# A decoder block on one core: the pooling gate's projection as seven block products, and loads pinned to program order

## The chip, the cores and the metric

One of the eight cores of one Trainium2 chip runs the whole kernel. The metric is the device time of one execution in microseconds (us). All data are 32-bit floats.

## The reference

The layer takes x (1024 rows of 1024), normalises it to h, projects h by one wide matrix and runs two branches, attention and pooling. The change sits in the pooling branch:

```
h = rms_norm(x, norm_gain) * (1 + scale) + shift         # scale, shift, gate from c
q, k, v, z_a, u, z_b, m_a, m_b = split(h @ w_in)         # eight blocks of 1024 columns
attn   = stick_breaking_attention(q, k, v)               # 16 heads, strictly causal
p_a    = (attn * silu(z_a)) @ w_branch_a
# pooling: trailing mean over 2, 4, 8 or 16 rows (by group of 256 channels) minus the row itself
d      = (cs - cs_shift) / count - u
p_b    = ((d @ pool_w) * pool_scale * silu(z_b)) @ w_branch_b
merged = sigmoid(m_a) * p_a + sigmoid(m_b) * p_b
out    = rms_norm(x + gate * (merged @ w_out), final_gain)
```

The kernel multiplies `pool_w` into the weights of u beforehand, so its `d` is already the pooled value before scale and gate.

## The kernel before

**Stages.** TensorE (PE) works through stages in this order: u (the pooled branch's input, weights already mapped), v, m (for m_b), z (for z_b), b (the product with `w_branch_b`), then attention with the remaining projections woven in, then the two output products. A float product is made of three products of split operands: high by high, high by low, low by high. ScalarE (ACT) casts the high half (fp32r), VectorE (DVE) subtracts it from the source to get the low half, so that each operand block costs one ACT cast and one DVE subtraction before PE can use both halves.

**`seven`.** A 1024x1024x1024 product in 2x2 blocks takes eight block products. Stages v, m and b use a scheme of seven: products p1 to p7 of sums and differences of blocks, 48 matmuls each (4 row tiles x 2 halves q x 2 x 3), into PSUM "chains" of four banks: a chain keeps accumulating over several products (p1, p6, p7, p4 in one; p5, p3 in another; p2 alone). The order of the products is p1, p5, p6, p7, p4, p3, p2. `raw` loads an operand block half (512 KB, two buffers of tag "raw" and two of tag "ar"); `a_s1`, `a_s3`, `a_s4` form the sums on DVE; `a_op` and `b_op` split into halves; `copied` and `added` take partial sums out of PSUM; `final(m, n, j, src)` hands over tile j of output block (m, n): (1,1) after p7, (1,0) after p4, (0,1) after p3, (0,0) after p2. In stage v, `values` casts the tile to halves (tile `vo`, three buffers) and stores it to DRAM `v_d`; in m, `gate_b` applies a sigmoid (tile `sb`) and stores to `sb_d`; in b, `branch` stores to `pb_d`.

**Stage z.** `project` runs z_b as eight column tiles of 48 matmuls (names `wzb`), 384 in all. Beside each tile j, the loop loads `u_d[j]`, forms the trailing-window difference (`load_u`, `make_d`: one to four window additions, one subtraction, two tiny edge operations), multiplies it with silu(z) (`silu`), forms the differences of quarters that stage b needs (t1, t2), and adds one eighth of the modulation gate: a load `wg` of `w_gate` and one DVE product with the row `sg` = silu(c).

**What sets the order.** Each engine runs its instructions strictly in a fixed order. A scheduler picks that order when the program is built, from its own estimates; `tc.keep_in_program_order` forbids it to put an instruction ahead of the one written before it on the same engine. SyncE (SP) issues nearly all transfers, one after the other: a transfer that waits for a semaphore holds back all behind it. In stages v, m, z and b no transfer is pinned before the change, and nothing on PE is.

Of the kernel before, what the change touches and what calls it, by code (L numbers as in the profile page):

```python
# [9 lines left out]
F32 = mybir.dt.float32  # L10
# [5 lines left out]
P = 128  # L16
# [35 lines left out]
def block_kernel(ctx, tc, a, out):  # L52
# [3 lines left out]
    def pool(name, **kw):  # L56
        return tc.tile_pool(name=name, bufs=1, reuse_waits="tile", **kw)
# [9 lines left out]
    def bank(tag, name):  # L67
        return psp.tile([P, 512], F32, tag=tag, bufs=BANKS[tag], name=name)
# [463 lines left out]
    dhls = {}  # L532

    def load_u(j):
        u = dif.tile([P, S + 16], F32, tag="u", bufs=2, name=f"u{j}")
        v.memset(u[:, S:], 0.0)
        nc.sync.dma_start(u[:, :S], u_d[j])
        return u

    def make_d(j, u):  # L540
        win = WINDOWS[j // 2]
        cur, n, step = u, S + 16, 1
        while step < win:
            nxt = dif.tile([P, S + 16], F32, tag="win", bufs=2, name=f"win{j}_{step}")
            n -= step
            v.tensor_add(nxt[:, :n], cur[:, :n], cur[:, step:step + n])
            cur, step = nxt, 2 * step
        t0 = S - win + 1
        d = dif.tile([P, S], F32, tag="d", bufs=5, name=f"d{j}")
        v.scalar_tensor_tensor(d[:, :t0], cur[:, :t0], 1.0 / win, u[:, :t0], ALU.mult, ALU.subtract)  # L550
# [21 lines left out]
    def added(t, src):  # L572
        v.tensor_add(t, src, t)
        return t

    def seven(nm, sums, load, b_of, a_moves, ta, tb, final, direct):

        s2k = sums.tile([P, 4, 512], F32, tag="s2k", bufs=1, name=nm + "s2k")

# [30 lines left out]
            return t  # L610

        chain, keep = {}, {}
        for name in ("p1", "p5", "p6", "p7", "p4", "p3", "p2"):
            c = {"p5": "b", "p3": "b", "p2": "c"}.get(name, "a")
# [14 lines left out]
            for j in range(4):  # L629
                if name == "p1":  # L630
                    keep["s1", j] = copied("s1", 4, j, ps[j])
                elif name == "p6":
                    keep["s2", j] = copied("s2", 4, j, ps[j])
                elif name == "p7":
                    final(1, 1, j, added(copied("s3", 4, j, ps[j]), chain["b"][j]))
                elif name == "p4":
                    final(1, 0, j, ps[j] if direct else copied("s3", 4, j + 4, ps[j]))
                elif name == "p3":
                    final(0, 1, j, added(keep["s2", j], ps[j]))
                elif name == "p2":  # L640
                    final(0, 0, j, added(keep["s1", j], ps[j]))

    with ExitStack() as vps:

        vp = vps.enter_context(pool("vp"))

        tq = [vp.tile([P, 4, 512], F32, name=f"ht{i}") for i in range(4)]

        def hq(k, n, q):
            sl = slice(4 * k + 2 * q, 4 * k + 2 * q + 2), slice(512 * n, 512 * n + 512)  # L650
            return [t[:, sl[0], sl[1]].bitcast(F32) for t in (h_hi, h_lo)]

        def difference(dst, x, y, name):
            tmp = vp.tile([P, 2, 512], F32, tag="tmp", bufs=1, name=name)
# [19 lines left out]
        for i in reversed(range(KB)):  # L674
# [15 lines left out]

        def loads(w):
            def load(t, m, k, q):
                nc.sync.dma_start(t.rearrange("p k c -> p (k c)"), a[w][m, 2 * k + q])
            return load

        def values(m, n, j, src):
# [8 lines left out]
            )  # L705

        def gate_b(m, n, j, src):
            t = vs.tile([P, 512], F32, tag="go", bufs=3, name=f"sb{4 * m + j}_{n}")
            act.activation(t, src, AF.Sigmoid)
# [5 lines left out]
    turns[0] = cycle(("av", "tr", "pj", "z"))  # L715
    diffs = ExitStack()
    dif = diffs.enter_context(pool("dif", side="right"))

    pbs = ExitStack()
    pb = pbs.enter_context(pool("pb"))  # L720
    gb = pb.tile([P, KB, S], F32, name="gb")
    t1 = pb.tile([P, 4, 512], F32, name="t1")
    t2 = pb.tile([P, 4, 512], F32, name="t2")
    gate = pb.tile([P, KB], F32, name="gate")
    bias = pb.tile([P, KB], F32, name="gbias")
    nc.sync.dma_start(bias, a["b_gate"])
    sg = pb.tile([P, D], F32, name="sg")

    def part(src, k, n, q):
        return src[:, 4 * k + 2 * q:4 * k + 2 * q + 2, 512 * n:512 * n + 512]  # L730

    for j in range(KB):
        if j not in dhls:
            make_d(j, load_u(j))

        def silu(sh, ps):
            z = gb[:, j, sh * 512:sh * 512 + 512]
            act.activation(z, ps, AF.Silu)
            v.scalar_tensor_tensor(z, dhls[j][:, sh * 512:sh * 512 + 512], psc_v[:, j:j + 1], z, ALU.mult, ALU.mult)

        project(CZB + j, f"wzb{j}", silu, act, v)
        if j < 4:
            v.tensor_sub(t1[:, j], gb[:, j, 512:], gb[:, j, :512])
        else:
            v.tensor_sub(t2[:, j - 4], gb[:, j, 512:], t1[:, j - 4])
            v.tensor_sub(gb[:, j - 4, 512:], gb[:, j, 512:], gb[:, j - 4, 512:])
        if j == 0:
            nc.sync.dma_start(sg, a["c_row"].broadcast_to([P, D]))
            act.activation(sg, sg, AF.Silu)
        wg = pb.tile([P, D], F32, tag="wg", bufs=1, name=f"wg{j}")  # L750
        nc.sync.dma_start(wg, a["w_gate"][j])
        v.scalar_tensor_tensor(wg, wg, 1.0, sg, ALU.mult, ALU.mult, accum_out=gate[:, j:j + 1])
        del dhls[j]
    v.tensor_add(gate, gate, bias)
    nc.sync.dma_start(g_d[0].rearrange("(k p) -> p k", p=P), gate)
    diffs.close()

    sums = pbs.enter_context(pool("sums", side="right"))

    def load_b_w(t, m, k, q):  # L760
        r0 = (4 * k + 2 * q) * P
        nc.sync.dma_start(t, a["w_branch_b"][r0:r0 + 2 * P, 512 * m:512 * m + 512].rearrange("(k p) c -> p k c", p=P))

    def g_parts(name, q):
        if name in ("p5", "p6"):
            src = k2(t1 if name == "p5" else t2, q)
        elif name == "p4":
            src = k2(t2, q)
            v.tensor_sub(src, part(gb, 1, 0, q), src)
        else:  # L770
            src = part(gb, *dict(p1=(0, 0), p7=(0, 1), p3=(1, 1), p2=(1, 0))[name], q)
        return b_op(src, pb, 3, f"{name}b{q}")
# [10 lines left out]
    with pool("at") as at:  # L783
# [439 lines left out]
```

## Time and profile before

| | us |
|---|---|
| three runs | 1189.05, 1190.29, 1190.63; median 1190.29 |
| the profiled execution, device time | 1187.59 |
| its span, first to last instruction | 1185.8 |
| stage v in it | 129 to 205 |
| stage m | 205 to 281 |
| stage z | 281 to 368 |
| stage b | 368 to 445 |

Two views matter below. Groups of instructions give, for each line and kind, the count, the total busy time and the mean of one in ns, then the engine's idle time just before and what ended it. The list of transfers gives, for each, the queue that issues it, the count, its size and the median time from issue to landing. "SPq" is SP as an issuer of transfers. A matmul's mean (390 ns) is its length in the pipeline; the total divided by the count is what one adds.

### The profile page before, as it was taken

The numbers are of one execution on the slowest core, as the hardware profiler recorded it, in microseconds if no ns is written. First come the engines' busy times: TensorE is split into PE (matmuls) and PEld (weight loads), VectorE is DVE, ScalarE is ACT, GpSimd is POOL, SyncE is SP. The second block draws the span as 40 slices with busy tenths as digits, with TensorE's granted clock in tenths as the row PEclk, the third lists the DMA queues.
The fourth block names the chain that finished last, engine by engine and source line by source line (L and its number), as shares of the span: only waits on it lengthen the run. The fifth ranks groups of instructions, "written<-read, shape, count | busy, mean of one in ns | idle before, by whom it ended". The sixth has DMA issues, their size and how long they took to land.

```text
span 1185.8 us, 15373 instructions
## 1 busy us (share of the span) xinstructions
PE 1169.2 (99%) x5602; PEld 975.0 (82%) x5602; DVE 832.4 (70%) x1072; ACT 588.3 (50%) x1137; POOL 216.7 (18%) x248
## 2 busy tenths in 40 slices
PE   8999999999999999999999999999999999999997
PEld 7888888888888887888888888887888888888876
DVE  5767467555996651878788788879787973894653
ACT  5561355454313532667666666666666764232111
POOL 1000000000000004124234242443343622000001
PEclk9999999999999999999999999999999999999999
DMA  9651529546535257322333142423333126984622
GB/s 349 257 193 62 180 103 318 187 162 234 200 103 176 97 179 222 79 81 91 84 98 90 62 121 54 135 62 103 94 88 99 37 72 208 349 280 157 213 70 73
DMA packets 74750, 172.49 MB, mean 145 GB/s; under 512 B 9393, under 2 KB 22833, under 8 KB 72498
## 3 DMA queue, kind: packets, MB, share of 16 engines
q1 hardware_dynamic: 68770, 160.82, 41.6%
q10 hardware_dynamic: 5904, 10.68, 2.5%
q8 instruction: 44, 0.72, 0.3%
q14 instruction: 32, 0.26, 0.1%
HBM read 121.14 MB, written 33.56 MB: 130 GB/s over the span
## 4 chain that ended last, share of the span: by engine, by line
PE 84%; DVE 7%; DMA 3%; issue 3%; ACT 2%; SPq 0%; POOL 0%; POOLq 0%; DVEq 0%; ACTq 0%
PE p L101 24%; PE wzb L101 7%; PE mp L101 6%; PE vp L101 6%; PE bp L101 6%; PE o L101 6%; PE pa L101 5%; PE u L101 5%; PE z L101 5%; PE av L101 4%; PE wt L101 4%; PE ua L101 3%; DVE om L942 2%; DVE be L101 2%; PE wm L101 1%
## 5 line engine op out<-in xcount | busy, mean ns | idle before, releaser
L101 PE MATMUL p<-hT,w 128*128 128x512 f32 x1536 | 392.7, 392 | 1.3 <-DVE klo L101 1.3
L101 PEld LDWEIGHTS p<-hT,w 128*128 128x128 f32 x1536 | 283.0, 188 | 59.5 <-DVE klo L101 1.7
L942 DVE TENSOR_TENSOR_SCAN om<-om,eye 128x511 f32<-128x511 f32 (+7 forms) x128 | 184.0, 1442 | 68.9 <-ACT om L938 68.3
L149 POOL TENSOR_TENSOR w<-w_raw,w 128x256 fp32r<-128x256 f32 x124 | 124.8, 1037 | 571.5 <-ACT w L146 571.5
L938 ACT ACTIVATE om<-z 128x512 f32<-128x512 f32 (+2 forms) x192 | 95.0, 495 | 109.2 <-PE z L101 46.8
L962 DVE TENSOR_TENSOR wt<-wt,wt 128x512 fp32r<-128x512 f32 (+1 forms) x160 | 99.0, 619 | 15.7 <-ACT wt L961 14.7
L101 PE MATMUL av<-wt,vv 128*128 128x512 f32 x320 | 106.0, 412 | 0.1
L961 ACT CAST wt<-wt 128x512 fp32r<-128x512 f32 (+1 forms) x160 | 88.2, 551 | 35.0 <-PE wt L101 34.8
L101 DVE TENSOR_TENSOR be<-be,om 128x512 f32<-128x512 f32 (+7 forms) x128 | 98.5, 775 | 0.0
L101 PE MATMUL wt<-ident,be 128*128 128x128 f32 x576 | 90.3, 274 | 3.9 <-DVE wt L962 3.1
L939 ACT ACTIVATE be<-z 128x512 f32<-128x512 f32 (+2 forms) x192 | 94.0, 489 | 0.0
L101 PE MATMUL pa<-ga,wa 128*128 128x512 f32 x384 | 89.9, 390 | 0.9 <-DVE s L1115 0.8
L101 PE MATMUL o<-wo,mhl 128*128 128x512 f32 (+1 forms) x408 | 89.6, 377 | 0.0
L101 PE MATMUL wzb<-hT,wzb 128*128 128x512 f32 x384 | 87.2, 389 | 0.0
L101 PEld LDWEIGHTS pa<-ga,wa 128*128 128x128 f32 x384 | 71.9, 188 | 16.5 <-issue 1.2
L101 PEld LDWEIGHTS o<-wo,mhl 128*128 128x128 f32 x408 | 73.5, 188 | 14.1
L101 PEld LDWEIGHTS wt<-ident,be 128*128 128x128 f32 x576 | 69.5, 140 | 18.7 <-DVE wt L962 6.2
L101 PEld LDWEIGHTS wzb<-hT,wzb 128*128 128x128 f32 x384 | 72.1, 188 | 15.0
L991 POOL TENSOR_TENSOR tp<-tp,tl 128x256 f32<-128x256 f32 x32 | 38.1, 1190 | 153.9 <-DVE tp L988 153.9
L101 PE MATMUL z<-kl,q 128*128 128x512 f32 (+2 forms) x192 | 65.5, 341 | 0.0
L101 PE MATMUL z<-kh,q 128*128 128x512 f32 (+2 forms) x192 | 64.1, 334 | 0.0
L101 PE MATMUL u<-hT,wg 128*128 128x512 f32 x240 | 55.5, 391 | 0.0
(265 smaller groups left out, 1650.0 us busy)
## 6 DMA issues: line engine op xcount, KB each, us to landing
w_raw<-in_w_in SPq DMA_DIRECT2D x32, 512.0 KB, 3.5
v_d<-vo SPq DMA_DIRECT2D x16, 512.0 KB, 4.2
vv<-v_d SPq DMA_DIRECT2D x8, 1024.0 KB, 6.3
wa_raw<-in_w_branch_a SPq DMA_DIRECT2D x16, 512.0 KB, 4.7
wa<-in_w_mod SPq DMA_DIRECT2D x7, 1024.0 KB, 7.4
kh<-kh SPq DMA_DIRECT2D x48, 128.0 KB, 2.3
va<-in_w_v SPq DMA_DIRECT2D x10, 512.0 KB, 4.0
ma<-in_w_mb SPq DMA_DIRECT2D x10, 512.0 KB, 4.4
```

Source lines behind the costliest of these rows:

```text
L101: ins = op(*args, **kw)
L149: gp.tensor_tensor(hl[:, 1, es], raw[:, es], hl[:, 0, es].bitcast(F32), op=ALU.subtract)
L938: act.activation(om[:, 1 + b0:1 + b0 + n], zp[:, :n], AF.Sigmoid, scale=-0.125)
L939: act.activation(be[:, b0:b0 + n], zp[:, :n], AF.Sigmoid, scale=0.125)
L942: v.tensor_tensor_scan(om[:, 1:W], om[:, 1:W], eye[:, :W - 1], 0.0, ALU.mult, ALU.max)
L961: act.copy(wt[:, 0, :off], pt[:, :off])
L962: v.tensor_sub(wt[:, 1, :off], pt[:, :off], wt[:, 0, :off].bitcast(F32))
L991: gp.tensor_add(tp, tp, tl)
```

## The change

1. Stage z becomes a call of `seven` with the weights laid out for it (`w_zb`), and `gate_z` as its `final`. The silu output goes to four quarter tiles `gq`; three of them reuse tiles of differences of h whose last product is done.
2. The order of the seven products becomes p1, p2, p5, p6, p7, p4, p3 in all four stages, so that block (0,0) is handed over second and (0,1) last; p2 takes the four banks that p5 takes after it. All stages use the same banks for the same chains.
3. The pooling differences are made in stages v and m, one after each of four products (`beside`), and stored to a new DRAM tensor `d_d` through GpSimd's queue (POOL); `gate_z` loads them back by tiles `ds` (three buffers).
4. The modulation gate's eight parts go beside the products of stage z.
5. `held` pins the loads of weights, of u and of `w_gate` to program order on SP; so are the stores of `branch` and the loads of v in attention.
6. `sb` has two buffers where it had three.

The diff, cut:

```
+    def held(dst, src):
+        tc.keep_in_program_order(nc.sync.dma_start(dst, src))
 def load_u(j):
-        nc.sync.dma_start(u[:, :S], u_d[j])
+        held(u[:, :S], u_d[j])
 def make_d(j, u):
...
-        dhls[j] = d
+        gp.dma_start(d_d[j], d)
-    def seven(nm, sums, load, b_of, a_moves, ta, tb, final, direct):
+    def seven(nm, sums, load, b_of, a_moves, ta, tb, final, direct, beside={}):
...
-        for name in ("p1", "p5", "p6", "p7", "p4", "p3", "p2"):
+        for name in ("p1", "p2", "p5", "p6", "p7", "p4", "p3"):
...
-                chain[c] = [bank((tb if c == "b" else ta)[j // 2], f"{nm}{name}_{j}") for j in range(4)]
+                chain[c] = [bank((ta if c == "a" else tb)[j // 2], f"{nm}{name}_{j}") for j in range(4)]
...
+            for do in beside.get(name, ()):
+                do()
...
             def load(t, m, k, q):
-                nc.sync.dma_start(t.rearrange("p k c -> p (k c)"), a[w][m, 2 * k + q])
+                held(t.rearrange("p k c -> p (k c)"), a[w][m, 2 * k + q])
...
-        seven("v", vs, loads("w_v"), h_parts("v"), True, ("av", "tr"), ("pj", "z"), values, True)
-        seven("m", vs, loads("w_mb"), h_parts("m"), False, ("pj", "z"), ("av", "tr"), gate_b, True)
+        seven("v", vs, loads("w_v"), h_parts("v"), True, *banks, values, True, pooled(p1=(3,), p6=(2,), p7=(1,), p3=(0,)))
+        seven("m", vs, loads("w_mb"), h_parts("m"), False, *banks, gate_b, True, pooled(p1=(7,), p6=(4,), p7=(6,), p3=(5,)))
+        diffs.close()
...
-        project(CZB + j, f"wzb{j}", silu, act, v)
+            def gate_z(m, n, j, src):
+                ct = 4 * m + j
+                ds = zg.tile([P, 512], F32, tag="ds", bufs=3, name=f"ds{ct}_{n}")
+                nc.sync.dma_start(ds, d_d[ct][:, 512 * n:512 * n + 512])
+                z = gq[m, n][:, j]
+                act.activation(z, src, AF.Silu)
+                v.scalar_tensor_tensor(z, ds, psc_v[:, ct:ct + 1], z, ALU.mult, ALU.mult)
...
+            def modulated(j):
+                wg = zg.tile([P, D], F32, tag="wg", bufs=1, name=f"wg{j}")
+                held(wg, a["w_gate"][j])
+                v.scalar_tensor_tensor(wg, wg, 1.0, sg, ALU.mult, ALU.mult, accum_out=gate[:, j:j + 1])
+            where = dict(p1=(0, 1), p6=(2,), p7=(3, 4), p4=(5,), p3=(6, 7))
+            seven("z", vs, loads("w_zb"), h_parts("z"), False, *banks, gate_z, True, ...)
...
+        seven("b", vs, load_b_w, g_parts, False, *banks, branch, False)
```

Three places show how the order of instructions moves. In the names, `va`, `ma`, `za`, `ba` are the loads of operand blocks of stages v, m, z, b (a11, a12, a21, a22, with `s` or `d` for the copies used in sums; the digit behind is the half q), and the last number counts tiles.

First place, SP in stage v. Before, around the end of p7 and p4:

```order
L693 DMA va22_0_1405<-in_w_v 128x1024
L693 DMA va22_1_1437<-in_w_v 128x1024
L693 DMA va12s_0_1485<-in_w_v 128x1024
L702 DMA v_d_75<-vo4_1_1380 128x4x256
L702 DMA v_d_75<-vo5_1_1387 128x4x256
L693 DMA va12s_1_1515<-in_w_v 128x1024
L702 DMA v_d_75<-vo6_1_1394 128x4x256
L702 DMA v_d_75<-vo7_1_1401 128x4x256
```

The loads of p4 (va22) and p3 (va12s) stand ahead of most of the stores of p7's results. Now, around the end of p2:

```order
L577 DMA va12_1_1213<-in_w_v 128x1024
L712 DMA v_d_75<-vo0_0_1243 128x4x256
L712 DMA v_d_75<-vo1_0_1248 128x4x256
L712 DMA v_d_75<-vo2_0_1253 128x4x256
L712 DMA v_d_75<-vo3_0_1258 128x4x256
L577 DMA va21_0_1266<-in_w_v 128x1024
L577 DMA va22_0_1268<-in_w_v 128x1024
L577 DMA va11s_0_1271<-in_w_v 128x1024
```

The loads for p5 (va21, va22, va11s) stand behind the four stores of p2's results; the same pattern follows p7, p4 and p3.

Second place, SP at the change from stage m to stage z. Before:

```order
L693 DMA ma12_1_2145<-in_w_mb 128x1024
L129 DMA wzb0_raw_2215<-in_w_in 128x1024
L710 DMA sb_d_76<-sb0_1_2097 128x512
L710 DMA sb_d_76<-sb1_1_2101 128x512
L710 DMA sb_d_76<-sb2_1_2105 128x512
L710 DMA sb_d_76<-sb3_1_2109 128x512
L129 DMA wzb1_raw_2290<-in_w_in 128x1024
```

The first weights of stage z are loaded before the stores of p3's results of m. Now:

```order
L720 DMA sb_d_76<-sb3_1_2292 128x512
L577 DMA u5_2295<-u_d_78 128x1024
L744 DMA gbias_2319<-in_b_gate 128x8
L746 DMA sg_2321<-in_c_row 128x1024
L577 DMA za11_0_2329<-in_w_zb 128x1024
L577 DMA za11_1_2358<-in_w_zb 128x1024
```

The first weights (za11) stand behind the last store of stage m, the load of u5 and the load of `sg`, whose place in memory was the differences' work space: it waits for the difference of u5. ACT now has, behind m's last sigmoid:

```order
L719 ACTIVATE sb3_1_2292<-ms2_3_2015 128x512
L747 ACT_TABLE_LOAD
L747 ACTIVATE sg_2321<-sg_2321 128x1024
L559 CAST zp1a0_2331<-za11_0_2329 128x1024
L559 CAST zp1a1_2360<-za11_1_2358 128x1024
```

The cast of the first weights stands behind the table load and silu of `sg`.

Third place, SP at the change from stage z to stage b. Before:

```order
L129 DMA wzb7_raw_2755<-in_w_in 128x1024
L537 DMA u6_2659<-u_d_78 128x1024
L751 DMA wg7_2816<-in_w_gate 128x1024
L762 DMA ba11_0_2830<-in_w_branch_b 128x2x512
L537 DMA u7_2739<-u_d_78 128x1024
L755 DMA g_d_74<-gate_2201 128x8x1
```

The first weights of b (ba11) go ahead of the store of the finished gate `g_d`. Now:

```order
L737 DMA ds3_1_2897<-d_d_79 128x512
L577 DMA wg6_2901<-in_w_gate 128x1024
L577 DMA wg7_2904<-in_w_gate 128x1024
L758 DMA g_d_74<-gate_2318 128x8x1
L577 DMA ba11_0_2919<-in_w_branch_b 128x2x512
L577 DMA ba11_1_2951<-in_w_branch_b 128x2x512
```

They stand behind both last parts of the gate (one buffer `wg`) and behind the store of the finished gate.

More of the change, by code (lines that the diff above doesn't have):

```diff
@@ L81, in block_kernel @@
     u_d = dram.tile([KB, P, S], F32, name="u_d")
+    d_d = dram.tile([KB, P, S], F32, name="d_d")
     ident = idp.tile([P, P], F32, name="ident")
@@ L548, in make_d @@
         t0 = S - win + 1
-        d = dif.tile([P, S], F32, tag="d", bufs=5, name=f"d{j}")
+        d = dif.tile([P, S], F32, tag="d", bufs=2, name=f"d{j}")
         v.scalar_tensor_tensor(d[:, :t0], cur[:, :t0], 1.0 / win, u[:, :t0], ALU.mult, ALU.subtract)
@@ L653, in difference @@
         def difference(dst, x, y, name):
-            tmp = vp.tile([P, 2, 512], F32, tag="tmp", bufs=1, name=name)
+            tmp = tmpp.tile([P, 2, 512], F32, tag="tmp", bufs=1, name=name)
             v.tensor_sub(dst, x[0], y[0])
@@ L679, in block_kernel @@
         early.close()
+        tmps.close()
         vs = vps.enter_context(pool("vs", side="right"))
+        diffs = ExitStack()
+        dif = diffs.enter_context(pool("dif", side="right"))
         def h_parts(nm):
@@ L707, in gate_b @@
         def gate_b(m, n, j, src):
[L708 removed]
+            t = vs.tile([P, 512], F32, tag="go", bufs=2, name=f"sb{4 * m + j}_{n}")
             act.activation(t, src, AF.Sigmoid)
             nc.sync.dma_start(sb_d[4 * m + j][:, 512 * n:512 * n + 512], t)
[L712 to L713 removed]
@@ L715, in block_kernel @@
[L715 to L739, printed above, removed]
-        project(CZB + j, f"wzb{j}", silu, act, v)
[L742 to L747, printed above, removed]
+        banks = ("av", "tr"), ("pj", "z")
@@ new lines, in pooled @@
+        def pooled(**where):
+            return {name: [lambda j=j: make_d(j, load_u(j)) for j in js] for name, js in where.items()}
+        seven("v", vs, loads("w_v"), h_parts("v"), True, *banks, values, True, pooled(p1=(3,), p6=(2,), p7=(1,), p3=(0,)))
+        seven("m", vs, loads("w_mb"), h_parts("m"), False, *banks, gate_b, True, pooled(p1=(7,), p6=(4,), p7=(6,), p3=(5,)))
+        diffs.close()
+        gp_ = vps.enter_context(pool("gp_", side="right"))
+        gq = {(0, 0): gp_.tile([P, 4, 512], F32, name="g00"), (1, 1): tq[0], (1, 0): tq[1], (0, 1): tq[2]}
@@ new lines, in block_kernel @@
+        with pool("zg", side="right") as zg:
+            def gate_z(m, n, j, src):
[5 more added lines that the diff above has]
+                v.scalar_tensor_tensor(z, ds, psc_v[:, ct:ct + 1], z, ALU.mult, ALU.mult)
+            gate = zg.tile([P, KB], F32, name="gate")
+            bias = zg.tile([P, KB], F32, name="gbias")
+            nc.sync.dma_start(bias, a["b_gate"])
+            sg = zg.tile([P, D], F32, name="sg")
@@ L748, in block_kernel @@
             nc.sync.dma_start(sg, a["c_row"].broadcast_to([P, D]))
             act.activation(sg, sg, AF.Silu)
[L750 to L772, printed above, removed]
@@ new lines, in block_kernel, with load_b_w @@
+            seven("z", vs, loads("w_zb"), h_parts("z"), False, *banks, gate_z, True,
+                  {name: [lambda j=j: modulated(j) for j in js] for name, js in where.items()})
+            v.tensor_add(gate, gate, bias)
+            nc.sync.dma_start(g_d[0].rearrange("(k p) -> p k", p=P), gate)
+        t1 = tq[3]
+        bt = vps.enter_context(pool("bt", side="right"))
+        t2 = bt.tile([P, 4, 512], F32, name="t2")
+        def load_b_w(t, m, k, q):
+            r0 = (4 * k + 2 * q) * P
+            held(t, a["w_branch_b"][r0:r0 + 2 * P, 512 * m:512 * m + 512].rearrange("(k p) c -> p k c", p=P))
@@ new lines, in g_parts @@
+        def g_parts(name, q):
+            g00, g01, g10, g11 = (k2(gq[k, n], q) for k, n in ((0, 0), (0, 1), (1, 0), (1, 1)))
+            x, y = k2(t1, q), k2(t2, q)
+            if name == "p5":
+                v.tensor_sub(x, g01, g00)
+            elif name == "p6":
+                v.tensor_sub(y, g11, x)
+            elif name == "p7":
+                v.tensor_sub(g01, g11, g01)
+            elif name == "p4":
+                v.tensor_sub(y, g10, y)
+            return b_op(dict(p1=g00, p2=g10, p5=x, p6=y, p7=g01, p4=y, p3=g11)[name], vs, 2, f"b{name}b{q}")
@@ L847, in load_v @@
         def load_v(p):
-            nc.sync.dma_start(pair[p]["vv"].rearrange("p b h i d -> p (b h i d)").bitcast(F32), v_d[p].rearrange("p b c -> p (b c)"))
+            tc.keep_in_program_order(
+                nc.sync.dma_start(pair[p]["vv"].rearrange("p b h i d -> p (b h i d)").bitcast(F32), v_d[p].rearrange("p b c -> p (b c)")))
         def use_za(p, sh, ps):
```

13 lines of the change are left out of this document (7 added, 6 removed).

## The prediction, made before the changed kernel was run

> **What bounds the kernel now.** I read the busy table by stretches first, then the groups of matmuls, SP's waits, the landing times, and last the rows of ACT and DVE that a new chain would be made of. Stages v, m, z and b stand in this order below; columns are PE, weight loads, DVE, ACT, POOL.
>
> ```profile
> span 1185.8 us, 15373 instructions
> 129.00:205.00 76.00, 76.00 (x337) 62.94 (x336) 51.70 (x55) 37.94 (x50) 0.00 (x0) 1.00 0.65 218
> 205.00:281.00 76.00, 76.00 (x337) 62.91 (x336) 43.10 (x44) 36.27 (x48) 0.00 (x0) 1.00 0.53 180
> 281.00:368.00 87.00, 87.00 (x385) 72.06 (x384) 72.98 (x106) 22.91 (x30) 0.00 (x0) 1.00 0.52 170
> 368.00:445.00 77.00, 77.00 (x338) 63.14 (x338) 49.20 (x48) 34.78 (x43) 2.84 (x4) 1.00 0.45 155
> L101 PE MATMUL wzb<-hT,wzb 128*128 128x512 f32 x384 | 87.2, 389 | 0.0
> L101 PE MATMUL mp<-hT,mp1a 128*128 128x512 f32 x48 | 11.0, 389 | 0.0
> ```
>
> PE never waits in these four stages: every microsecond there is matmuls, 87.2/384 = 0.227 us each, and a product of `seven` lasts 48 x 0.227 = 10.9. So a matmul taken out is worth 0.227, and any wait that appears counts in full. DVE has the least room, in stage z.
>
> **What is taken out and what is moved.** Stage z drops from 384 matmuls to 7 x 48 = 336: 48 x 0.227 = 10.9 us off. DVE's work moves. Per difference:
>
> ```profile
> L546 DVE TENSOR_TENSOR win<-win 128x1037 f32<-128x1037 f32 (+2 forms) x12 | 14.8, 1233 | 0.1
> L550 DVE SCALAR_TENSOR_TENSOR d<-win,u 128x1023 f32<-128x1023 f32 (+3 forms) x8 | 9.7, 1217 | 0.1
> L739 DVE SCALAR_TENSOR_TENSOR gb<-d,vecs,gb 128x512 f32<-128x512 f32 x16 | 11.9, 746 | 7.5 <-ACT gb L738 7.5
> L752 DVE SCALAR_TENSOR_TENSOR wg<-wg,sg 128x1024 f32<-128x1024 f32 x8 | 9.8, 1221 | 0.6 <-DMA wg<-in_w_gate 0.5
> ```
>
> Stage v gets 6 window additions and 4 subtractions, 6 x 1.23 + 4 x 1.22 = 12.3: 64 of 76 us. Stage m gets 14 and 4, 22.1: 65 of 76. Stage z has m's 43.1 of operand work plus 11.9 and 9.8: 65 of 76. DVE stays under PE everywhere, so its load alone costs nothing; PE's matmuls cover it. The eight stores of d go through POOL, idle in these stages; the trace shows no transfer from POOL. Nothing needs them before the reload of `ds`, over 20 us later, so I take 0, with 0 to 5 us as bounds (5 is about the slowest 512 KB row below, `u`).
>
> **What is added: loads behind stores.** SP holds back everything behind a transfer that waits: in the trace it stood 29.7 us before one load of v.
>
> ```profile
> SPq L693 <- PE u L101: 29.7, 1, 29.7
> v_d<-vo SPq DMA_DIRECT2D x16, 512.0 KB, 4.2
> va<-in_w_v SPq DMA_DIRECT2D x10, 512.0 KB, 4.0
> ma<-in_w_mb SPq DMA_DIRECT2D x10, 512.0 KB, 4.4
> sb_d<-sb SPq DMA_DIRECT2D x16, 256.0 KB, 2.8
> u<-u_d SPq DMA_DIRECT2D x8, 512.0 KB, 4.7
> wg<-in_w_gate SPq DMA_DIRECT2D x8, 512.0 KB, 4.0
> ba<-in_w_branch_b SPq DMA_DIRECT2D x10, 512.0 KB, 3.9
> ba12s<-in_w_branch_b SPq DMA_DIRECT2D x2, 512.0 KB, 3.6
> sg<-in_c_row SPq DMA_DIRECT2D x1, 512.0 KB, 6.7
> ```
>
> In the new order the loads of p5, p4, p3 and of the next stage's p1 stand behind the stores of the product just finished. Before, they left some ten microseconds earlier. PE's next product therefore waits for a chain: result out of PSUM, store, load, sum, cast. Its links:
>
> ```profile
> L573 DVE TENSOR_TENSOR vs<-vp,vs 128x512 f32<-128x512 f32 x12 | 8.1, 685 | 0.9 <-PE vp L101 0.6 <-ACT vs L609 0.3
> L609 ACT COPY vs<-vp 128x512 f32<-128x512 f32 x12 | 7.1, 588 | 8.1 <-PE vp L101 8.0
> L700 ACT CAST vo<-vs 128x512 fp32r<-128x512 f32 x12 | 7.4, 622 | 10.5 <-DMA v_d<-vo 5.1 <-DVE vs L573 4.7 <-DVE vo L701 0.7
> L701 DVE TENSOR_TENSOR vo<-vs,vo 128x512 fp32r<-128x512 f32 x12 | 8.1, 687 | 1.0 <-ACT vo L700 0.8
> L709 ACT ACTIVATE sb<-ms 128x512 f32<-128x512 f32 x12 | 7.4, 632 | 6.9 <-DVE ms L573 6.0 <-DMA sb_d<-sb 0.9
> L587 DVE TENSOR_TENSOR ma<-ma,ma 128x1024 f32<-128x1024 f32 x2 | 2.4, 1222 | 1.5 <-DMA ma<-in_w_mb 1.5
> L559 ACT CAST vp5a<-va 128x1024 fp32r<-128x1024 f32 x2 | 2.1, 1050 | 0.0
> 202.33 0.69 DVE L573 TENSOR_TENSOR vs<-vp,vs 128x512 f32<-128x512 f32 x1 [0.41 <-PE vp L101]
> 203.10 0.62 ACT L700 CAST vo<-vs 128x512 fp32r<-128x512 f32 x1 [2.43 <-DVE vs L573]
> 128.88 0.33 SPq L693 DMA_DIRECT2D va<-in_w_v  x1
> ```
>
> The two timeline rows give a hand-over of 0.1 us (202.33 + 0.69 to 203.10); I take 0.2 behind PE, and 0.35 for each issue on SP (0.33 in the last row).
>
> One transition in full, v's p2 to p5, in us from p2's last matmul. Its first bank is done at -2.7 (three banks times four matmuls remain). DVE adds until -1.8, ACT casts until -1.1, DVE's low half until -0.3, store out at -0.2, landed at 4.0. The fourth tile needs that buffer back (`vo` has three): cast until 4.7, low half 5.5, store 5.6, then va21 at 5.95 and va22 at 6.3, landed 10.3; DVE sum 11.6, cast 12.8, PE starts at **12.9**.
>
> The others by the same links:
> - v, p7 to p4: ACT's copy and DVE's addition come first, then the same buffer wait; store at 5.8, u1, va22 landed 10.5, cast 11.6. DVE, in its own order, does u1's window and subtraction before the low half: **12.8**. p4 to p3, straight from PSUM: store 3.4, load landed 7.65, DVE difference, cast: **10.2**. p3 to m's p1, with u0's load between: **11.1**. Sum 47.0.
> - m has two `sb` buffers and 2.8 us stores: **11.2**, **11.2**, **9.1**. m to z: last store at 2.6, u5 landed 7.7, three windows and the subtraction until 12.9, only then `sg`, landed 19.7; table load, silu and the cast of za11 follow on ACT, 1.3 + 1.1 + 1.1: **23.2**. Sum 54.7.
> - z: `ds` has three buffers, so ds3 waits for the first gate product, and za21 for ds3: **7.5**. p7 to p4: ds and two `wg` parts of one buffer stand ahead, load out at 6.6: **12.1**. p4 to p3: **7.1**. z to b: wg6's product ends at 6.2, wg7 lands 10.3, product, `g_d`, ba11 out at 12.2, landed 16.1, cast: **17.2**. Sum 43.9.
> - b: **8.2**, **7.1**, **7.3**. Sum 22.6. The end of b keeps the next weights ahead of its stores and costs nothing new.
> - p5 to p6: the late halves of p5 and a window push DVE's low halves 2.2 us late in v and m, under 1 in z and b: 5.3.
>
> The two rows behind the table load and silu:
>
> ```profile
> 283.29 1.28 ACT L738 ACT_TABLE_LOAD   x1
> 292.01 1.06 ACT L749 ACTIVATE sg<-sg 128x1024 f32<-128x1024 f32 x1 [4.31 <-DMA sg<-in_c_row]
> ```
>
> Waits: 47.0 + 54.7 + 43.9 + 22.6 + 5.3 = 173.5 us, in 15 gaps of 7 to 23 us.
>
> **What a gap does to PE.** The trace has no gap like these; the one near these stages is 1.26 us long, and the 20 matmuls behind it take 4.84 us, 0.24 each, as before. The other bound is the start of the kernel, where PE comes from rest:
>
> ```profile
> L101 PE MATMUL idle<-ident,ones 128*128 128x128 f32 x20 | 4.6, 429 | 1.5 <-POOL x L220 1.5
> L101 PE MATMUL wm<-praw,wt 128*128 128x256 f32 x32 | 7.1, 379 | 0.0
> 2.00:4.00 2.00, 2.00 (x11) 2.00 (x11) 0.17 (x1) 0.01 (x1) 0.12 (x4) 1.00 0.68 217
> 457.32 4.84 PE L101 MATMUL p<-hT,w 128*128 128x512 f32 x20 [1.26 <-DVE klo L101]
> ```
>
> Per column of the same kind of matmul: 4.6/(20 x 128) = 1.80 ns at the start, 7.1/(32 x 256) = 0.87 later. So the first 4.6 us ran at about half rate and lost 2.4 us, although the granted clock in that stretch reads 1.00. A restart after a gap costs between 0 and 2.4. Gaps of 7 us and more are nearer to rest than to 1.26 us, but one sample of the start doesn't fix how long the slow phase is; I take 2.0, so 15 x 2.0 = 30.
>
> [...]
>
> **The sum**, against the profiled execution: 1187.6 - 10.9 + 173.5 + 30 = 1380.2. That execution is 2.7 below the median of the runs shown, so on their scale 1383.
>
> **Rivals.**
> 1. Gaps as worked out, but PE restarts at full rate: 1353. For it: the clock column at 1.00 throughout. Against: the first 4.6 us.
> 2. Shorter waits. Stores and loads run on emptier queues than the medians, the chains overlap better: at 5 us per gap, 75 + 15 = 90 in place of 203.5, 1270. Against: a load issued at 128.88 with the queue nearly empty had its sum on DVE no earlier than 133.23, the medians again.
>
> ```profile
> 133.23 1.22 DVE L587 TENSOR_TENSOR va<-va,va 128x1024 f32<-128x1024 f32 x1
> ```
>
> 3. The other side, faster: the loads do not really wait, and pacing only spreads DVE's work. Then only the 10.9 is left: 1179. It decides where a load leaves at least 4.0 + 1.2 + 1.05 = 6.3 us before the end of the product ahead. Against: each of these loads is pinned behind stores that need that product's last bank.
> 4. Longer: DVE, at 65 of 76 us, is held by transfers in its own order (window additions wait for u, gate parts for `wg`) and adds some 3 us to each gap: 1430.
>
> **Chances.** As worked out 0.68; rival 1 0.16; rival 2 0.07; rival 3 0.03; rival 4 0.06. The predicted time is the first's, 1383. The range, 1325 to 1412: the low end is rival 1 with each gap 1.9 us shorter (1353 - 28), the high end the full 2.4 us restart and 1.5 us more per gap (1383 + 6 + 23). By 0.2%, about what a measurement of this kernel can tell: faster 0.03, the same 0.01, slower 0.96.
>
> **What would show it.** Right: gaps of PE in front of p5, p4, p3 and the next p1, ended by ACT's cast or DVE, with SP waiting for `vo` and `sb` just before; the longest ahead of z's p1 and b's p1; p2 and p7 without gaps; stage z's matmuls at 336; a higher mean per matmul in the first product after a gap if rest slows PE. Wrong: PE busy through stages v and m. The forecast fails if SP's issue order on the chip is not the one shown, or if landing times fall far below their medians.

## The result and the profile after

The changed kernel takes 1390.3 us (median of four runs, 1387.2 to 1392.7) against 1189.7 for the kernel before on the same chip: a ratio of 1.169, 95% interval 1.166 to 1.172. The forecast was 1383, slower.

The page of the profiled execution (device time 1392.74):

```profile
span 1391.0 us, 15406 instructions
PE 1195.0 (86%) x5554; PEld 988.4 (71%) x5554; DVE 868.8 (62%) x1100; ACT 612.9 (44%) x1163; POOL 223.3 (16%) x256
PEclk9999896888878886888999999999999999999999
```

Slices 5 to 19 of the third row are the four stages: the clock is down where the prediction's rows of the stages have it at 1.00. By stages v, m, z, b (columns as in the prediction):

```profile
128.76:261.75 132.99, 84.01 (x337) 67.36 (x336) 62.28 (x72) 40.36 (x52) 1.07 (x2) 0.82 0.44 151
261.75:397.72 135.97, 86.08 (x337) 68.86 (x337) 66.56 (x75) 41.33 (x52) 2.66 (x5) 0.81 0.38 140
397.72:539.01 141.29, 86.80 (x337) 69.60 (x337) 71.28 (x82) 38.78 (x50) 0.00 (x0) 0.80 0.36 123
539.01:650.32 111.31, 85.46 (x337) 68.71 (x338) 50.43 (x47) 35.67 (x43) 2.82 (x4) 0.85 0.35 119
sum 521.56, PE 342.35 PEld 274.52 DVE 250.56 ACT 156.13 POOL 6.55; mean PE 85.59 PEld 68.63 DVE 62.64 ACT 39.03 POOL 1.64
```

Before, the four stages were 316 us and PE was busy in all of them. Now they are 521.6, and the spans differ by 1391.0 - 1185.8 = 205.2: nothing outside these stages changed. Of 521.6, PE is busy 342.4 and waits 179.2. Matmuls at the old pace would be 28 x 10.88 = 304.6, so 37.7 us more than that are spent in matmuls. Most of it, 34.4, is in the 15 products behind the gaps, which last 12.6 to 14.0 us each where the undisturbed ones last 11.04; nearly all the rest is the end of the pipeline that each gap leaves uncovered (11.04 - 10.88 = 0.16 us each). The forecast had 173.5 of waits and 30 of slow restarts.

PE's waits, the longest and the shortest of the 15 gaps (us in total, times, longest), and then SP's longest waits:

```profile
PE bp L102 <- ACT bp1a L559: 25.1, 1, 25.1
PE zp L102 <- ACT zp1a L559: 20.0, 1, 20.0
PE vp L102 <- ACT vp5a L559: 13.5, 1, 13.5
...
PE bp L102 <- ACT bp4a L559: 7.1, 1, 7.1
SPq L712 <- DVE vo L711: 108.0, 16, 33.5
SPq L720 <- ACT sb L719: 89.3, 16, 26.2
```

The gaps stand ahead of p5, p4 and p3 in every stage and ahead of the p1 of m, z and b, and the 15 add up to 176.0; p2 and p7 have none. The other 3.2 us of waiting stand ahead of p6. SP stands before the stores of `v_d` (line 712) and `sb_d` (720), and the loads stand behind it. One chain in the timeline, v from p2 to p5 (start, duration, then in brackets the wait and what ended it):

```profile
150.22 4.81 SPq L712 DMA_DIRECT2D v_d<-vo  x4
153.31 0.62 ACT L710 CAST vo<-vs 128x512 fp32r<-128x512 f32 x1 [1.86 <-DMA v_d<-vo]
155.09 1.64 SPq L577 DMA_DIRECT2D va<-in_w_v  x2
161.79 1.23 DVE L590 TENSOR_TENSOR va<-va,va 128x1024 f32<-128x1024 f32 x1 [7.15 <-DMA va<-in_w_v]
163.10 1.04 ACT L559 CAST vp5a<-va 128x1024 fp32r<-128x1024 f32 x1 [9.17 <-DVE va L590]
164.19 1.22 PE L102 MATMUL vp<-vp5a,vp5b 128*128 128x512 f32 x2 [13.52 <-ACT vp5a L559]
```

Three stores, the first of their three buffers given back for the fourth, its store, load, sum, cast, PE. Behind that gap, stretches of the clock (the figure behind POOL's column):

```profile
164.00:166.00 2.00, 1.80 (x4) 1.49 (x5) 1.42 (x2) 0.14 (x1) 0.00 (x0) 0.50 0.90 279
166.00:167.00 1.00, 1.00 (x4) 0.73 (x3) 0.45 (x1) 0.00 (x0) 0.00 (x0) 0.50 0.76 258
167.00:168.00 1.00, 1.00 (x6) 0.84 (x5) 0.77 (x1) 0.15 (x1) 0.00 (x0) 0.89 0.91 324
168.00:170.00 2.00, 2.00 (x10) 1.67 (x9) 0.37 (x1) 0.90 (x1) 0.00 (x0) 1.00 1.06 385
```

PE restarts at half rate and keeps it for some 3 us: four matmuls in the first 1.8 us, where nearly eight fit at 0.227 us each, and four in the next microsecond; the granted clock reads 0.50 until 167, 0.89 in the next microsecond, and 1.00 from 168 on.

### The profile page after: what moved, and what is told of

The parts are those of the page before. It is cut to its first block, busy times and chain, and to the rows that moved or that the text cites. A ratio compares the mean times of both kernels' runs of the same rounds, so it can differ in the third digit from the quotient of the medians.

```text
span 1391.0 us, 15406 instructions
## 1 busy us (share of the span) xinstructions
PE 1195.0 (86%) x5554; PEld 988.4 (71%) x5554; DVE 868.8 (62%) x1100; ACT 612.9 (44%) x1163; POOL 223.3 (16%) x256
## 4 chain that ended last, share of the span: by engine, by line
PE 70%; DMA 11%; DVE 10%; ACT 4%; issue 3%; SPq 1%; POOL 0%; POOLq 0%; ACTq 0%; DVEq 0%
PE p L102 21%; PE pa L102 6%; PE o L102 5%; PE zp L102 5%; PE bp L102 5%; PE vp L102 5%; PE mp L102 5%; PE z L102 4%; PE av L102 4%; PE u L102 4%; PE wt L102 4%; PE ua L102 2%; DVE om L949 2%; DMA ba<-in_w_branch_b 2%; DMA za<-in_w_zb 1%
## 5 line engine op out<-in xcount | busy, mean ns | idle before, releaser
L969 DVE TENSOR_TENSOR wt<-wt,wt 128x512 fp32r<-128x512 f32 (+1 forms) x160 | 99.0, 619 | 16.5 <-ACT wt L968 15.6
L102 PEld LDWEIGHTS o<-wo,mhl 128*128 128x128 f32 x408 | 73.5, 188 | 14.1
L554 POOL DMA_DIRECT2D d_d<-d x8 | 4.5, 562 | 318.1 <-DVE d L553 170.7
L102 PEld LDWEIGHTS u<-hT,wg 128*128 128x128 f32 x240 | 44.8, 188 | 10.3 <-ACT wg L102 0.8
```

The costliest lines, as they stand in the source:

```text
L102: ins = op(*args, **kw)
L554: gp.dma_start(d_d[j], d)
L969: v.tensor_sub(wt[:, 1, :off], pt[:, :off], wt[:, 0, :off].bitcast(F32))
```

## The experiments

**1. Are the held loads the cause?** The loads are set free; everything else of the change stays.

```diff
 def held(dst, src):
-    tc.keep_in_program_order(nc.sync.dma_start(dst, src))
+    nc.sync.dma_start(dst, src)
```

> The changed kernel with one word taken out: the loads of the four staged products, of u and of the gate weights are no longer held in program order (the stores of stage b and the reloads of v stay held). Theory (program order puts each load behind the stores of the product before it, and PE waits for the chain store, load, sum, cast): the loads move ahead, nearly all of the 176 us of waits and the 33 us of slow restarts go, a few short ones stay where a load still stands behind three v_d stores; 1190 us, between 1177 and 1215. Rival A (the order of the products or DVE's added work makes the waits): 1360 to 1390, the gaps ahead of p5, p4 and p3 stay. Rival B (the transfers themselves are too slow or too many): 1300 or more, with loads that land late though they were issued early.

Measured: 1197.2 us against 1187.9, ratio 1.007 (1.006 to 1.009). The order of products, DVE's added work, the seven products of z and the stores of d are all still there, and 193 us are gone. That refutes both rivals. Of the gaps one is left:

```profile
PE mp L102 <- ACT mp3a L559: 9.4, 2, 8.5
284.07 0.60 ACT L719 ACTIVATE sb<-mp 128x512 f32<-128x512 f32 x1 [8.20 <-DMA sb_d<-sb]
291.02 1.21 ACT L719 ACTIVATE sb<-mp 128x512 f32<-128x512 f32 x2 [6.35 <-DMA sb_d<-sb]
```

It is none of the kind forecast. ACT waited for the two buffers of `sb`, until their stores landed. One had been issued at 273.5 and one at 276.9, the store of `g_d` between them at 275.4, and they took 10.6 and 14.1 us where such a store has a median of 2.8 in the kernel before and 2.0 in the changed one. Experiments 5 and 8 return to that.

**2. Does holding alone do it, without the rest?** The kernel before, with the weight loads of v, m and b held (in both loads, as here).

```diff
-  nc.sync.dma_start(t.rearrange("p k c -> p (k c)"), a[w][m, 2 * k + q])
+  tc.keep_in_program_order(nc.sync.dma_start(t.rearrange("p k c -> p (k c)"), a[w][m, 2 * k + q]))
```

> The kernel before, with the weight loads of v, m and b held in program order and nothing else changed: the old order of products, no windows in v and m, stage z as it was. Theory (the holding alone makes the gaps): a gap ahead of p4, p3, p2 and the next stage's p1 in v (44 us), ahead of p4, p3 and p2 in m (27) and in b (23), 94 us, and 10 restarts of 2.2: 1187.6 + 94 + 22 = 1304, between 1285 and 1330. Rival (it needs the new order, or the work that came into v and m): under 1200.

Measured: 1315.0 us (one run). Ten gaps, ahead of p4, p3, p2 and m's p1 in the old order, the longest and the shortest:

```profile
PE vp L101 <- ACT vp4a L559: 11.5, 1, 11.5
PE bp L101 <- ACT bp2a L559: 7.0, 1, 7.0
```

They sum to 87.4 (94 forecast); shorter waits of 4.0 ahead of v's p1 and 2.9 ahead of b's p5 came on top. Holding is enough; the new order and the moved work are not needed for it.

**3. What does a held load wait for?** Loads held as in the change; the result stores of v, m and b are issued by ACT (those of `pb_d` lose their pin with that).

```diff
-            nc.sync.dma_start(          # v_d; likewise sb_d and pb_d
+            nc.scalar.dma_start(
```

> The changed kernel with its loads still held in program order, but with the result stores of v, m and b (v_d, sb_d, pb_d) issued by ACT and not by SP; stage z is left as it is for comparison. Theory (what a held load waits for is the stores ahead of it on SP): the gaps inside v, m and b go, also that ahead of m's p1; z's p1 falls to 5 to 10, z's p5, p4 and p3 stay at about 9, 13 and 7.5, b's p1 at about 25: 1187.6 - 10.9 + 62 + 5 x 2.2 + 3 = 1253, between 1235 and 1270. Rival (the loads or DVE's sums are late by themselves, the stores are only neighbours): 1340 or more, the gaps in v, m and b stay.

Measured: 1260.6 us (one run). All gaps of 7 us and more inside v, m and b are gone, those ahead of z's p5, p4 and p3 and of b's p1, where the queue was left alone, are about where they were:

```profile
PE bp L102 <- ACT bp1a L559: 25.7, 1, 25.7
PE zp L102 <- ACT zp1a L559: 13.3, 1, 13.3
PE zp L102 <- ACT zp4a L559: 12.3, 1, 12.3
PE zp L102 <- ACT zp5a L559: 9.4, 1, 9.4
PE zp L102 <- ACT zp3a L559: 6.8, 1, 6.8
```

So in v, m and (from p2 on) b, where no wait of PE above 1.2 us is left, it was not the holding that cost the time but what stood ahead of the held load on the same queue. z's p1 fell to 13.3, less than I expected (5 to 10): its weights still stand behind `sg`.

**4. Is it enough to write the loads one product earlier?** All loads stay held, but those of the next product, and its sums, are written ahead of the finals of the running one, across stages too; `g_d` is stored by POOL.

```diff
+            now = [a_of[names[i_ + 1]](q) for q in range(2)]   # raw loads and sums of the next product
             for j in range(4):
                 if name == "p1":                               # the finals of this product
```

> The changed kernel with all loads held in program order as before, but the loads and sums of each next product written ahead of the finals of the product that runs (across the ends of the stages too), and the store of g_d issued by POOL. Theory (not the holding as such, but the place in the program at which it holds, costs the time): no gaps of 7 us or more are left, and the 48 matmuls fewer in z show: 1187.6 - 10.9 + a few us of short waits, 1180, between 1176 and 1195. Rival A (holding costs by itself, because loads are held by their buffers and hold up the stores): 1220 or more, the waits are now those of vo, sb and ds. Rival B (DVE's load in v, m and z is too much without the gaps): 1195 to 1215, PE waits for DVE.

Measured: 1240.5 us, ratio 1.043 (1.041 to 1.045). My expectation was wrong; the time is rival A's, and one of its waits, that for `vo`, is there. Six gaps of 2.9 to 9.9 us are left. The longest is ahead of z's p2: ACT waits 5.5 us for the load of `sg` before it casts p2's weights. The next, 8.7 us ahead of b's p5, is the store of `g_d` again (see 5). The one ahead of v's p3, 7.4 us:

```profile
190.68 0.99 SPq L577 DMA_DIRECT2D u<-u_d  x1
191.76 1.65 SPq L577 DMA_DIRECT2D va12s<-in_w_v  x2
193.58 10.23 SPq L731 DMA_DIRECT2D v_d<-vo  x4
201.38 0.59 ACT L729 CAST vo<-vp 128x512 fp32r<-128x512 f32 x1 [4.74 <-DMA v_d<-vo]
201.86 1.99 ACT L559 CAST vp3a<-va12s 128x1024 fp32r<-128x1024 f32 x2
```

The load of p3 goes out at 191.8, since p7's four stores and the held load of u stand ahead of it. The stores of p4 in turn come late, ACT waits for a `vo` buffer until 201.4, and only behind that in its order stands the cast for p3. A product lasts 10.9 us; the chain of stores, a load, a window of DVE and a cast took 16.3, from the first of p7's stores at 185.5 to the cast at 201.9.

**5. The longest gap.** Ahead of b's p1 the forecast had 17.2 and the trace has 25.1. Until the load of ba11 the chain ran nearly as worked out: it went out 10.8 us behind z's last matmul, 12.2 forecast. Then it took 13 us to land in place of 3.9:

```profile
524.29 0.38 SPq L758 DMA_DIRECT2D g_d<-gate  x1
524.76 15.85 SPq L577 DMA_DIRECT2D ba<-in_w_branch_b  x3
537.91 1.04 ACT L559 CAST bp1a<-ba 128x1024 fp32r<-128x1024 f32 x1 [22.57 <-DMA ba<-in_w_branch_b]
```

Ahead of it stands the store of `g_d`: 4 KB, written as 1024 pieces of 4 bytes (the profile counts 1088 packets under 512 bytes between 520 and 540). In the trace of before the same store, issued at 343.2, took this long to land, with no other transfer issued behind it until 351.4:

```profile
g_d<-gate SPq DMA_DIRECT2D x1, 4.0 KB, 11.7
```

Two experiments move that store to another queue, and change its form:

```diff
-            nc.sync.dma_start(g_d[0].rearrange("(k p) -> p k", p=P), gate)
+            gp.dma_start(g_d[0].rearrange("(k p) -> p k", p=P), gate)          # 5: POOL's queue
```
```diff
+            turned = bank("pj", "turned")[:KB, :P]                             # 5b: 8 rows of 512 bytes
+            transpose(turned, gate)
+            rows = zg.tile([KB, P], F32, name="rows")
+            act.copy(rows, turned)
+            nc.sync.dma_start(g_d[0].rearrange("(k p) -> k p", p=P), rows)
```

> The changed kernel with the store of g_d (4 KB written as 1024 pieces of 4 bytes) issued by POOL and not by SP, nothing else changed. In the changed kernel the gap ahead of b's p1 was 25.1 us against 17.2 forecast: the load ba11 right behind that store took 13 us to land in place of 3.9. Theory A (loads behind it on SP's queue wait for its pieces): on another queue it does not hold them, the gap falls to 16 or 17, the span to 1382. Theory B (the pieces hold up the transfer engines for all queues, as it looked with the loads ahead, where the store was POOL's and loads issued 3 to 5 us behind it landed 12 us late): the gap stays at 22 to 26, the span at 1387 to 1392.

> The changed kernel with the gate turned by TensorE from 128 x 8 to 8 x 128 and copied by ACT before it is stored, so that g_d is 8 rows of 512 bytes on SP's queue in place of 1024 pieces of 4 bytes. If the small pieces are what delays ba11, by either theory, ba11 lands in 4 to 5 us: the gap ahead of b's p1 falls to 17 to 18 (1 us more for the turn and the copy), the span to 1383. Rival (any transfer behind the burst of stage z is that late): 25, no change.

Measured: span 1379.1 and 1379.7 (1391.0 in the profiled execution before the edit, which was the longest of four from 1385.4 on; device times 1380.9 and 1381.5, one run each). Both save 11 to 12 us against that execution and about 6 against the shortest of the four, for different reasons. With POOL's queue the gap is 11.7 us, since ba11 no longer waits on SP for the finished gate and goes out at 517.9, ahead of the store. But the next two loads of b, issued by SP at 525.8, 3 us behind POOL's store, were nearly as late as ba11 before, and PE waited 2.6 us ahead of b's p2. First the transfers of experiment 5 between 517 and 540 (count, size, median us from issue to landing; the loads of ba there are two early, 5.4, and two late, 11.3 to 11.4), then those of 5b with its two idle pieces of PE:

```profile
ba<-in_w_branch_b SPq DMA_DIRECT2D x4, 512.0 KB, 11.3
g_d<-gate POOLq DMA_DIRECT2D x1, 4.0 KB, 10.4
ba<-in_w_branch_b SPq DMA_DIRECT2D x4, 512.0 KB, 4.6
PE turned L102 <- DVE gate L757: 10.5, 1, 10.5
PE bp L102 <- ACT bp1a L559: 6.0, 1, 6.0
```

So theory B holds as far as the loads show it: those that SP issued 3 us behind POOL's store landed in 11.3 to 11.4 us, late on another queue as well; what the two queues share, no run shows. With rows in place of the pieces the loads land in 4.6, and the gap is 10.5 + 6.0 = 16.5, the turn of the gate between them, where the prediction had 17.2.

**6. The order of the products alone,** in the kernel before, with its banks and free loads.

```diff
-        for name in ("p1", "p5", "p6", "p7", "p4", "p3", "p2"):
+        for name in ("p1", "p2", "p5", "p6", "p7", "p4", "p3"):
```

> The kernel before with one part of the change alone: the seven products of v, m and b in the order p1, p2, p5, p6, p7, p4, p3 with the banks that belong to it; its loads are free, windows, stage z and queues are as before. Theory (the order by itself costs nothing): 1187 to 1191, ratio 0.999 to 1.002, PE busy through v, m and b. Rival (early results of p2 crowd DVE and the stores): 1195 or more, waits of a few us ahead of p5 and p6.

Measured: 1196.0 us (1192.7 to 1201.0), ratio 1.007 (1.005 to 1.010). The rival was right. In the profiled execution, the slowest of the five at 1201.0, PE waits 8.8 us in four places ahead of p5 and p6. Two of them:

```profile
PE bp L101 <- DVE bs L573: 3.4, 1, 3.4
PE mp L101 <- DVE mp6b L566: 1.9, 1, 1.9
```

The two kinds differ. The wait ahead of p6 is for an operand: its low half (line 566) comes late from DVE. The wait ahead of p5 ends with line 573, DVE's addition that takes p2's sum out of PSUM: in the new order p5 takes the four banks that p2 has just filled, so PE cannot start before DVE has emptied the first. The order costs some 9 us in the kernel before (6 to 12 by the interval). In the changed kernel the long gaps ahead of p5 hide most of that; 3.2 us were left ahead of p6.

**7. What does a restart cost?** The kernel before, with ACT held up ahead of 15 casts.

```diff
+        if times:
+            act.copy(hl[:, 0, 0], after)          # waits for the fourth bank of the product before
+            for _ in range(times - 1):
+                act.copy(hl[:, 0], src)
         act.copy(hl[:, 0], src)
```

> The kernel before with gaps of chosen length ahead of 15 products of v, m and b: ACT waits for the fourth bank of the product before, then copies the weights 1 to 12 times (1.05 us each) ahead of the cast that PE needs; nothing else is changed, the copies only repeat work. Gaps: v 1.3, 2.4, 3.4, 4.5, 5.5 us (p6, p7, p4, p3, p2), m 6.6, 7.6, 8.7, 10.8, 12.9, b 2.4, 3.4, 4.5, 5.5, 6.6 in the same places, 86 us in all. What is disputed is the slow phase behind a gap. In the changed kernel a product behind a gap of 7 to 25 us took 1.9 to 3.1 us more than its 10.9. Theory (any gap over some 3 us costs the same, between 1.5 and 3): about 12 slow products, 1187.6 + 86 + 26 = 1300, the granted clock at 0.50 for 3 to 6 us behind each, and none behind the gaps of 1.3 and 2.4. Rival (the loss grows with the gap): under 1 us behind 4 us, over 2.5 behind 13; 1287.

Measured: 1354.8 us (one run). The total is off, because the gaps are: 127.9 us and not 86, about 2.8 more each, as casts of the other operand and half stand behind the copies on ACT too. No gap shorter than 3.5 came out of it, and no run shows the bound of some 3 us that I expected: gaps of 1.7 to 2.1 us lost from 0.1 to 1.7 us in experiments 6, 8 and 9. But the ladder tells what a restart costs. The shortest and the longest gaps (the product's duration, and in brackets the gap; undisturbed it is 11.04, and 11.15 in b):

```profile
153.63 14.02 PE L101 MATMUL vp<-vp6a,vp6b 128*128 128x512 f32 x48 [3.56 <-ACT vp6a L563]
172.73 13.07 PE L101 MATMUL vp<-vp7a,vp7b 128*128 128x512 f32 x48 [5.07 <-ACT vp7a L563]
356.04 13.54 PE L101 MATMUL mp<-hT,mp3a 128*128 128x512 f32 x48 [12.78 <-ACT mp3a L563]
385.28 12.61 PE L101 MATMUL mp<-hT,mp2a 128*128 128x512 f32 x48 [15.69 <-ACT mp2a L563]
```

3.0 us lost behind 3.6, 2.0 behind 5.1, 2.5 behind 12.8, 1.6 behind 15.7. All 15 lie between 1.5 and 3.0, 35.3 together, 2.4 on average, and they do not grow with the gap: the rival falls. In the changed kernel the same measure gives 1.5 to 2.9, 2.3 on average, for gaps of 7 to 25 us. What sets the loss within that range, no run shows.

**8. The version without the two causes.** Loads free, `g_d` in rows (edits of 1 and 5b together).

> The changed kernel with its loads free, as in the first experiment, and with g_d stored as 8 rows of 512 bytes after a turn by TensorE. With free loads the one long gap was 8.5 us ahead of m's p3: ACT waited for sb buffers whose stores were issued 1.5 us behind g_d and landed 7 and 14 us later in place of 2. Theory (the small pieces caused that): the gap and its slow restart go, 1196.0 - 8.5 - 2.2 = 1185, against 1188 for the kernel before: ratio 0.996 to 0.999. Rival (the stores are late for another reason): 1193 to 1198.

Measured: 1187.5 us against 1187.2, ratio 0.9998 (0.9990 to 1.0007). The 8.5 us gap is gone, so it was the store of `g_d`. The rest of the change is worth nothing: the four stages take

```profile
128.24:446.00 317.76, 308.29 (x1347) 251.53 (x1346) 239.76 (x266) 156.07 (x200) 6.19 (x11) 1.00 0.66 217
```

317.8 us where they took 316. The 48 matmuls are saved, 10.9 us, but 317.8 - 308.3 = 9.5 us of short waits, mostly for DVE and up to 2.1 each, take their place, with 308.3 - 304.6 = 3.7 us more in the matmuls around them. This is not the half rate of a restart: the granted clock reads 1.00. The two longest waits are of the two kinds of experiment 6: 2.1 us ahead of v's p5, for a bank (line 573), and 1.8 ahead of z's p6, for a low half (line 566).

**9. Where do the short waits come from?** v and m go back to the old order of products, z and b keep the new one.

```diff
+        for name in ("p1", "p5", "p6", "p7", "p4", "p3", "p2") if late else ("p1", "p2", "p5", "p6", "p7", "p4", "p3"):
```

> The previous kernel (loads free, g_d in rows) with v and m back in the order p1, p5, p6, p7, p4, p3, p2 and their banks, z and b in the new order. The order alone cost the kernel before 8 us, in waits of 1.7 to 3.4 ahead of p5 and p6 in v, m and b; with free loads 6.6 us of short waits were left in v and m. Theory (these waits belong to the order, because p2's additions and stores come just when p5 and p6 need DVE): they go, 1187 - 5 = 1182, ratio 0.993 to 0.998. Rival (they belong to DVE's added windows): 1186 to 1192, the waits are only elsewhere.

Measured: 1191.7 us, ratio 1.003 (1.002 to 1.004). The rival was right: the waits are elsewhere. Ahead of v's p5 the wait for a bank (line 573) is gone, but waits of 1.0 to 2.1 us for operands stand ahead of v's p5 and p6 and m's p5. As in 8, three of v's differences stand among or ahead of p5's operands in DVE's order. I put that down to the free loads of u, which come early; 10 holds them.

**10. Holding in the right place.** As 9, with only the loads of u and of the gate weights held, and the work beside a product written ahead of that product's finals.

```diff
+            for do in beside.get(name, ()):
+                do()
             for j in range(4):
                 if name == "p1":
...
-            for do in beside.get(name, ()):
-                do()
```

> The same as the kernel with the old order in v and m, except that the loads of u and of the gate weights are held in program order, and written ahead of the finals of their product; the weights of the products stay free. Theory (pacing is harmless where the held load stands ahead of the stores, and it spreads DVE's windows): no gap of 4 us or more, 1178 to 1186, ratio 0.991 to 0.998. Rival (any held load is a barrier on SP's queue for the stores and loads around it): gaps of 5 us or more are back, 1195 or more.

Measured: 1184.7 us, ratio 0.997 (0.996 to 0.998), 0.3% below the kernel before. In the profiled execution, the slowest of the ten at 1188.3, v has no wait at all, and one of 3.5 us is left ahead of z's p5:

```profile
PE zp L102 <- DVE zs L573: 3.5, 1, 3.5
127.76:441.40 313.64, 309.28 (x1347) 253.71 (x1346) 242.38 (x272) 154.84 (x200) 6.56 (x11) 0.99 0.65 222
```

Here held loads do what pacing is for: the windows are spread over v and m. They are not quite free. The chain of the gap that is left:

```profile
299.26 0.41 SPq L580 DMA_DIRECT2D wg<-in_w_gate  x1
305.51 1.23 DVE L755 SCALAR_TENSOR_TENSOR wg<-wg,sg 128x1024 f32<-128x1024 f32 x1 [4.39 <-DMA wg<-in_w_gate]
306.67 0.69 DVE L573 TENSOR_TENSOR zs<-zp,zs 128x512 f32<-128x512 f32 x1
```

The one buffer of `wg` was free at 291.6, but its held load went out at 299.3, behind loads of z's weights that SP was waiting to issue. DVE waited 4.4 us for it, and p2's additions, which empty the bank that p5 takes, stood behind. Two things differ from 9 at once, the holding and the place ahead of the finals, and the same loads held behind the finals with free weights were not run; so that the place makes pacing cheap is argued and not shown.

## Why the prediction was right, point by point

**The mechanism** was right and is shown from both sides: free loads remove the gaps (1), held loads alone make them in the kernel before (2), and taking the stores off the queue removes the gaps whose loads stood behind those stores, all but 13.3 us ahead of z's p1, where `sg` stands in between as well (3).

**The sum.** Forecast against the profiled execution of before: -10.9 + 173.5 + 30 = 192.6. Measured, 205.2 by spans: -10.9, + 179.2 of waits, + 37 of slow restarts with the ends of the pipeline. (The medians differ by 200.6; the profiled execution of after was the slowest of its four, that of before, at 1187.6, was below all four of its own.) Of the 173.5, the 15 gaps were 168.2, and they came to 176.0.

- The term that was mis-sized is z to b: 17.2 forecast, 25.1 measured. The step that failed was "ba11 out at 12.2, landed 16.1", with the median landing of 3.9 us for a load that stood right behind a store of 1024 small pieces. The trace of before had a row that could have warned: that store took 11.7 us to land. The prediction gave it no time. With rows instead the gap was 16.5.
- m to z: 23.2 forecast, 20.0 measured. I had taken 6.7 us for `sg` from the trace of before; it landed in 5.1. And u5 was there 5.7 us behind m's last matmul, where the sum had 7.7.
- The other 13 gaps were forecast at 127.8 and came to 130.9; the one furthest off is b's p5, 10.4 for 8.2. Some of that is luck. In v's p2 to p5 the last store was out 4.4 us behind p2's end, earlier than worked out (5.6), because stores of `v_d` landed in 3.3 us (median) and not 4.2. The loads behind them took longer, `va` 6.0 and not 4.0, perhaps because they now leave in a burst, four within 2.2 us, which no run tested. Two errors of 1 to 2 us cancelled: 13.5 against 12.9.
- p5 to p6: 5.3 forecast, 3.2 measured (1.4 in v, 1.3 in m, 0.5 in b).
- Restarts: 2.0 forecast for each, 2.3 measured (34.4 / 15). Taking it from the slow start of the kernel was right; the bound of 2.4 at the upper end was not, single ones lose up to 2.9 here and 3.0 in experiment 7. At the start of the kernel the clock column read 1.00 beside matmuls at half rate (1.80 ns a column, 0.87 later); behind the gaps it does show the slow phase, at 0.50.

**What was costed at nothing.** POOL's stores of d: right as far as the runs show, experiment 10 has them and is faster than before. DVE under PE in every stage: right as a load (71.3 us in z where the sum gave 65; the differences of quarters for b, lines 772 to 776, stand in that stretch too), wrong in time. The order of products makes PE wait for DVE by 1.7 to 3.4 us ahead of p5 and p6 (6), partly because p5 takes p2's banks at once. The long gaps covered most of that in the changed kernel, and it shows once they are gone (8). The prediction's third rival, "Then only the 10.9 is left: 1179", would not have come out even with free loads: that kernel is 1197.2, and 1187.5 with `g_d` in rows.

**The rivals.** Full-rate restarts (1353) fall with the clock at 0.50. Shorter waits of 5 us (1270) and DVE held longer in its order (1430) did not occur; 13 of the 15 gaps lie within 2.3 us of the forecast.

## What to carry to other kernels

In these runs a load held in program order went out no earlier than the latest wait of anything ahead of it on its queue (in the changed kernel SP waited 108.0 us ahead of the stores of `v_d` and 89.3 ahead of those of `sb_d`, up to 33.5 at once), so ask of each held load which store stands ahead, what that store waits for, and whether the time left holds store, load, operand work and a restart of PE. Writing held loads ahead of the results of the running product is not enough by itself: with all loads held it still cost 4% (4), with only those held that pace DVE the kernel came out 0.3% ahead (10). If an order of products gives the next product the banks of the last, look whether PE waits until these are emptied (in experiment 6 3.4 us in b, 1.7 in m, nothing in v). When a small reshaping store goes out, look at what is in flight beside it: the 4 KB of `g_d` said little about what it cost its neighbours, 512 KB loads that landed in 11.3 us and more in place of 4.6.

## What the runs showed of the hardware that I had not expected

- A store of 4 KB in 1024 pieces of 4 bytes took 10.4 to 11.7 us to land and slowed transfers issued up to 4.5 us behind it, also from another queue: 512 KB loads landed in 11.3 to 14.4 us in place of 4.6, and a 256 KB store in 14.1 in place of 2.0 to 2.8 (medians). A 256 KB store issued 1.9 us ahead of it took 10.6 us (experiment 1); a load 2.0 us ahead of it in the kernel before took the usual 4.7. As 8 rows of 512 bytes it did not slow them: loads issued from 0.3 us behind it on landed in 4.1 to 4.9 (experiment 5b).
- A restart of PE cost 1.5 to 3.0 us in the changed kernel and in experiment 7, whether the gap was 3.6 or 25 us; behind the gap of 4.3 us in experiment 4 it was 3.2. Short gaps were not all safe: in experiment 6 the products behind gaps of 1.8 and 1.9 us lost 1.7 us each, with the clock at 0.50, and those behind 1.7 and, in experiment 8, 1.8 us lost 0.1. Two gaps of 2.1 us differ in the same way: ahead of v's p5 in experiment 8 the 32 matmuls behind it took 7.50 us where 7.41 is usual, and the clock was 1.000 as the mean of the whole execution; ahead of m's p5 in experiment 9 the next 16 took 5.36 us, where 16 x 0.227 = 3.63 is usual, so that some 1.7 us were lost. What decides between these was not tried.
